# Sharing out a first mixer's work anew: softmax division, conv taps, roots and modulation steps

## The chip, the cores and the metric

The kernel runs on one core of a Trainium2 chip. The metric is the device time of one execution in microseconds (us). The engines are named as the profile names them: PE is the matmul engine (PEld its weight loads), DVE the vector engine, ACT the scalar engine, POOL the GpSimd engine, and SP the engine whose queue issues nearly all DMAs here. Each engine works off its own queue in order; semaphores tie the queues together.

## The reference

Two layers of a diffusion trunk run over 128 context tokens and 512 latent tokens of width 1024, in float32. Layer 0 is a mixer of attention (8 heads, 2 key-value heads, width 64) and a convolution branch; layer 1 is an mLSTM; each is followed by a squared-ReLU MLP. Every sub-layer is modulated by vectors computed from a conditioning vector. What the change touches is the modulation vectors and the mixer of layer 0:

```
m = silu(cond) @ w_ada + b_ada            # 6 vectors of 1024 for each layer
h = x * (1 + scale) + shift
q, k, v, u = split(h @ w_in)              # 512, 128, 128, 1024 columns
q, k = rmsnorm(q), rmsnorm(k)             # per head of 64; latent tokens get rotary positions
p = softmax(q k^T / 8)                    # latent: over 512 latent and 128 cached context keys
att = p v
u = a * sigmoid(gate)                     # a, gate are the halves of u: 512 channels
u = depthwise_conv(u, width 31) + bias
u = silu(layernorm(u))
out = concat(att, u) @ w_out
```

## The kernel before

All products of float32 numbers run as three matmuls on a high and a low part (`mm3`, L193 to L195). Weights come from memory in raw tiles of 512 KB (L149, three buffers); a piece of 128x512 is split by a cast on ACT into `whi` (L166) and a subtraction on POOL into `wlo` (L167). The pairs of `whi` and `wlo` lie in a ring of eight slots.

The program is written with the Tile framework: the code fixes what is computed, and a scheduler with a model of the machine sets the order of each engine's queue when the kernel is built. The conv taps are written with a low priority (`CONV_BEHIND`), so they fill a queue where nothing else is ready.

The first mixer has two stages. In the products (58 to 193 us of the span) the projections are computed in the order of `GEMMS = "01k2qr3"`: glu 0 and 1, the key-value group, glu 2, the q group, the r group (the second half of q), glu 3. Each glu is 128 channels of the conv branch; behind it stand its 31 taps. A tap is either one DVE operation (L965; the first one L956) or an ACT product (L970) with a POOL addition (L972); `CONV_DVE` lists the taps that DVE takes, for four channel tiles of 128: all 31, all 31, eight, four. The k and q groups each have a chain on DVE (sum of squares, L1063; a reciprocal root; scaling, L1067; rotary positions, L1071 to L1080). The root is `rsqrt_here`: a guess from the exponent bits and three Newton rounds of four operations (L400 to L403), 15 operations on tiles of 128x10 or 128x20.

In the attention (193 to 335 us) twelve units (four pairs of heads, each with context tokens and two halves of the latent tokens) run one ahead: scores of the next unit (L1173, L1187), then the values of this one. A softmax is a maximum on DVE (L1152), an exponential with its sum on ACT (L1154), a reciprocal (L1155) and the division on DVE (L1157): 32 divisions of 128x640 and eight of 128x128. Transposes (L1219), their copies (L1222 on ACT, L1224 on DVE) and the products with v (L1226) follow. At unit 8 stands `conv_norm`, the layer norm of the conv branch, which uses the same root. Behind the attention comes out_proj.

A modulation vector is a generator, `ada_steps`: eight steps, each with two loads of 256 KB into a ring pair (L287) and four narrow matmuls into one PSUM bank (L293, which the trace shows as eight records of two kinds), then a DVE addition of the bias (L297) and, unless it is a gate vector, two PE transposes (L305) and four DVE copies (L308); a gate goes to memory (L300). The generators wait in a list, `pending`; `background(n)` runs the first of them n steps on, and `drain()` runs all that are left. Three vectors are queued in the products and seven in the attention, where `background` runs seven steps after each unit and `drain()` the rest at unit 8.

Of the kernel before, what the change touches and what calls it, by code (L numbers as in the profile page):

```python
# [9 lines left out]
F32 = mybir.dt.float32  # L10
F32R = mybir.dt.float32r
I32 = mybir.dt.int32
AF = mybir.ActivationFunctionType
# [5 lines left out]
P = 128  # L19
# [39 lines left out]
LATE_DVE = 0  # L59
CONV_DVE = (range(31), range(31), range(0, 31, 4), range(0, 31, 8))  # L60
PT_ACT = (0,)
# [6 lines left out]
GEMMS = "01k2qr3"  # L68
ADA_IN_ATT = 7
FAST = (1, 3)  # L70
# [22 lines left out]
def trunk_kernel(ctx: ExitStack, tc: tile.TileContext, I, O):  # L93
# [221 lines left out]
    def background(n=1):  # L315

        for _ in range(n):
            while pending:
                try:
# [3 lines left out]
                    pending.pop(0)  # L323

    def drain():
        while pending:
            background()
# [63 lines left out]
    def rsqrt_here(out, var, n, scale):  # L391
# [7 lines left out]
        for _ in range(3):  # L399
            nc.vector.tensor_tensor(out=a, in0=out, in1=out, op=ALU.mult)  # L400
            nc.vector.tensor_tensor(out=a, in0=a, in1=v, op=ALU.mult)
            nc.vector.tensor_scalar(out=a, in0=a, scalar1=-0.5, scalar2=1.5, op0=ALU.mult, op1=ALU.add)
            nc.vector.tensor_tensor(out=out, in0=a, in1=out, op=ALU.mult)  # L403

    def rsqrt_one(r, var):
# [507 lines left out]
    K.ada_raw = ring_raw  # L913
    pending += [ada_vec(0, v) for v in (2, 3, 4)]

    with ExitStack() as m0s:
# [13 lines left out]
        if True:  # L930
# [122 lines left out]
            def chain(x, c0, n):  # L1053
# [10 lines left out]
                rr = smallp.tile([P, NT, n], F32, name=f"rr{n}", bufs=1)  # L1064
                rsqrt_here(
                    rr.rearrange("p t h -> p (t h)"), ss.rearrange("p t h -> p (t h)"), NT * n, 1.0 / HD)
# [35 lines left out]
            def q_group(grp, kn=None):  # L1102
                ws = load_n256(w_in, grp * 256)
                for t in range(NT):
                    ps = ps1()
                    tm_tile(ws, act, t, ps[:, 0:256])
                    nc.scalar.copy(out=qkv[:, t, grp * 256:(grp + 1) * 256], in_=ps[:, 0:256])
                    background(1)
                    if kn is not None:
                        put_k(kn[:, t], t)  # L1110
                chain(0, grp * 256, 4)

            kn = None
            for what in GEMMS:
# [4 lines left out]
                else:  # L1119
                    glu(int(what), 3)  # L1120
            drain()
# [24 lines left out]

        def softmax(ps, dst, multi):

# [7 lines left out]
            d2 = dst.rearrange("p a b -> p (a b)") if multi else dst  # L1156
            nc.vector.tensor_scalar(out=d2, in0=d2, scalar1=ri[:, 0:1], scalar2=None, op0=ALU.mult)  # L1157

# [5 lines left out]
        def weights_of(i, s):  # L1164
# [3 lines left out]
            if s < 0:  # L1168
# [6 lines left out]
                for h in range(2):  # L1175
                    softmax(sp[:, h, 0:P], pp[:, h, :], False)
                Ps[i, s] = pp
                return
            pts = [[], []]
            for t in (1 + 2 * s, 2 + 2 * s):  # L1180
                for h in range(2):
# [7 lines left out]
                    pt = att.tile([P, 2, HT], F32, name="ptok", bufs=PTOK)  # L1189
                    softmax(s2[:, :, 0:HT], pt, True)  # L1190
                    pts[h].append(pt.rearrange("p a b -> p (a b)"))
# [44 lines left out]
        def conv_norm():  # L1236
# [35 lines left out]
            rc = smallp.tile([P, NT], F32, name="rc", bufs=1)  # L1272
            rsqrt_here(rc, pv[:, 0:NT], NT, 1.0)
            for ts in ((0, 1, 2, 3), (4,)):
# [21 lines left out]

        ada_late = [(0, 5)] + [(1, v) for v in range(6)]
        pending += [ada_vec(*x) for x in ada_late[:ADA_IN_ATT]]
        units = [(i, u) for i in range(HEADS // 2) for u in (-1, 0, 1)]
        prep(0)  # L1300
        weights_of(*units[0])
        for n, (i, u) in enumerate(units):
# [6 lines left out]
            if n == NORM_AT:  # L1309
                drain()  # L1310
                for t in range(NT):
# [3 lines left out]
                cl = cls.enter_context(tc.tile_pool(name="cl", bufs=1, side="right", reuse_waits="tile"))  # L1315
                conv_norm()
        cls.close()
    ada_scope.close()
# [80 lines left out]
    with Sub(0) as S:  # L1399
        S.rows(ALPHA)  # L1400
        out_proj(I["w_out_a"][0], S, S.finish_mixer("f0"))
        K.ada_m = lambda: S.fp.tile([P, 256], F32, name="ada_m")
        pending += [ada_vec(*x) for x in ada_late[ADA_IN_ATT:]]
        v_w = []
# [523 lines left out]
```

## Time and profile before

| | us |
|---|---|
| median of 3 runs | 1737.89 (1736.95 to 1741.92) |
| the profiled execution's own time | 1737.0 |
| its span in the trace | 1735.2 |
| products of the first mixer, in the span | 58 to 193 |
| attention | 193 to 335 |

The span reaches from the first to the last instruction that the trace shows. The view by windows gives each engine's busy time, the granted clock of PE and the share of the DMA engines in a stretch; the view by groups sums instructions of one line; the timelines list single instructions with the wait ahead of them and what ended it. A bracket such as `[6.61 <-DVE ada_m L297]` says that the engine stood idle for 6.61 us until DVE's write of `ada_m` by line 297. PE in the span's 40 slices is mostly at 8 or 9 tenths; the chain of waits that ended last begins at 898 us and so tells nothing of the first mixer.

### The profile page before, as it was taken

How to read it: one execution, taken by the hardware profiler on the slowest of the kernel's cores; microseconds unless marked ns; L12 is line 12 of the kernel's file. 1: busy time of each engine (PE TensorE's matmuls, PEld its weight loads, DVE VectorE, ACT ScalarE, POOL GpSimd, SP SyncE). 2: the span in 40 equal slices, each digit the busy share in tenths (PEclk: the TensorE clock that was granted, in tenths of full speed). 3: DMA queues.
4: the chain of work that ended last, by engine and by line, in shares of the span. 5: the costliest groups of instructions: out<-in, count | busy, mean ns of one | idle time of the engine just before them, and what ended most of it. 6: DMA issues, size and time to landing. Idle time of an engine off the chain costs nothing. (4 is left out here: it accounts for less than half of the span.)

```text
span 1735.2 us, 27401 instructions
## 1 busy us (share of the span) xinstructions
PE 1607.3 (93%) x10155; PEld 1412.7 (81%) x10155; DVE 1098.1 (63%) x1924; ACT 796.3 (46%) x1560; POOL 1005.4 (58%) x760
## 2 busy tenths in 40 slices
PE   7988899998989999999788998997989999999996
PEld 4678555898879989987678998897979889989885
DVE  2899997669434444356875687778498354344367
ACT  2224666345444344343543555556265444344343
POOL 2246474247955546548654766756459756546565
PEclk8999999998999999999999999999999999999998
DMA  9852885323432213216223222235442323213241
GB/s 307 256 185 75 268 306 178 71 101 119 130 85 92 92 56 97 86 61 206 83 69 103 71 84 91 98 98 194 123 152 85 125 89 98 89 57 98 85 158 61
DMA packets 151309, 211.76 MB, mean 122 GB/s; under 512 B 11845, under 2 KB 92969, under 8 KB 151176
## 3 DMA queue, kind: packets, MB, share of 16 engines
q1 hardware_dynamic: 150944, 209.94, 37.4%
q8 instruction: 80, 1.31, 0.3%
q14 instruction: 53, 0.43, 0.1%
q10 hardware_dynamic: 232, 0.08, 0.0%
HBM read 186.74 MB, written 23.24 MB: 121 GB/s over the span
## 5 line engine op out<-in xcount | busy, mean ns | idle before, releaser
L167 POOL TENSOR_TENSOR wlo<-raw,whi 128x512 fp32r<-128x512 f32 x374 | 518.6, 1410 | 412.2 <-ACT whi L166 397.5
L166 ACT CAST whi<-raw 128x512 fp32r<-128x512 f32 x368 | 224.7, 620 | 429.2 <-PE ps L195 192.1
L193 PE MATMUL ps<-whi,h 128*128 128x512 f32 x640 | 254.5, 399 | 11.0 <-DVE pr L526 5.7
L194 PE MATMUL ps<-wlo,h 128*128 128x512 f32 x640 | 254.6, 398 | 0.3 <-POOL wlo L167 0.3
L195 PE MATMUL ps<-whi,h 128*128 128x512 f32 x640 | 253.6, 396 | 0.0
L193 PE MATMUL ps<-act_h,whi 128*128 128x320 f32 (+2 forms) x704 | 221.2, 316 | 8.5 <-ACT act_h L625 7.5
L194 PE MATMUL ps<-act_l,whi 128*128 128x320 f32 (+2 forms) x704 | 221.3, 315 | 5.5 <-DVE act_l L626 3.1
L195 PE MATMUL ps<-act_h,wlo 128*128 128x320 f32 (+2 forms) x704 | 220.9, 314 | 2.2 <-POOL wlo L167 2.2
L167 POOL TENSOR_TENSOR wlo<-s,whi 128x512 fp32r<-128x512 f32 x118 | 163.9, 1393 | 67.2 <-ACT whi L166 61.9
L758 DVE TENSOR_TENSOR acc<-acc,ps 128x512 f32<-128x512 f32 x120 | 81.8, 685 | 162.0 <-PE ps L195 162.0
L193 PEld LDWEIGHTS ps<-whi,h 128*128 128x128 f32 x640 | 121.3, 190 | 40.2 <-DVE pr L526 6.0
L193 PEld LDWEIGHTS ps<-act_h,whi 128*128 128x128 f32 x704 | 135.3, 192 | 13.2 <-ACT act_h L625 7.9
L195 PEld LDWEIGHTS ps<-whi,h 128*128 128x128 f32 x640 | 121.3, 190 | 29.2
L194 PEld LDWEIGHTS ps<-wlo,h 128*128 128x128 f32 x640 | 121.5, 190 | 28.1 <-POOL wlo L167 1.2
L194 PEld LDWEIGHTS ps<-act_l,whi 128*128 128x128 f32 x704 | 134.9, 192 | 8.9 <-DVE act_l L626 3.9
L195 PEld LDWEIGHTS ps<-act_h,wlo 128*128 128x128 f32 x704 | 134.9, 192 | 3.1 <-POOL wlo L167 3.1
L193 PE MATMUL ps<-whi,act_h 128*128 128x256 f32 x440 | 126.1, 290 | 0.3 <-DVE acc L1095 0.3
L194 PE MATMUL ps<-wlo,act_h 128*128 128x256 f32 x440 | 124.7, 287 | 0.0
L195 PE MATMUL ps<-whi,act_l 128*128 128x256 f32 x440 | 123.8, 287 | 0.0
L972 POOL TENSOR_TENSOR cy<-cy,tap 128x655 f32<-128x655 f32 x50 | 80.3, 1606 | 54.0 <-DVE cy L965 22.6
L193 PE MATMUL ps<-T_h,whi 128*128 128x320 f32 x336 | 103.7, 309 | 1.6 <-ACT pr L550 1.6
L166 ACT CAST whi<-s 128x512 fp32r<-128x512 f32 x120 | 73.2, 616 | 67.3 <-DVE s L501 54.9
(437 smaller groups left out, 4066.0 us busy)
## 6 DMA issues: line engine op xcount, KB each, us to landing
raw<-in_w_ff_dram SPq DMA_DIRECT2D x128, 512.0 KB
whi<-in_w_ada_dram SPq DMA_DIRECT2D x80, 256.0 KB
wlo<-in_w_ada_dram SPq DMA_DIRECT2D x80, 256.0 KB
raw<-in_w_in_m_dram SPq DMA_DIRECT2D x32, 512.0 KB
ada_w<-in_w_ada_dram SPq DMA_DIRECT2D x32, 256.0 KB
acc_d<-acc SPq DMA_DIRECT2D x15, 512.0 KB
raw<-in_w_in_a_dram SPq DMA_DIRECT2D x12, 512.0 KB
rx<-acc_d SPq DMA_DIRECT2D x20, 256.0 KB
```

What stands on the lines that cost most here:

```text
L166: nc.scalar.copy(out=hv, in_=src)
L167: (eng or nc.gpsimd).tensor_tensor(out=lv, in0=src, in1=f32(hv), op=ALU.subtract)
L193: nc.tensor.matmul(out=out, lhsT=lh, rhs=rh, start=start, stop=False)
L194: nc.tensor.matmul(out=out, lhsT=lh, rhs=rl, start=False, stop=False)
L195: nc.tensor.matmul(out=out, lhsT=ll, rhs=rh, start=False, stop=stop)
L758: nc.vector.tensor_tensor(out=x, in0=x, in1=ps, op=ALU.add)
L972: nc.gpsimd.tensor_tensor(out=y, in0=y, in1=tp, op=ALU.add)
```

## The change

Four edits are made, all on the first mixer, and line numbers move by 1 to about 21.

- Of the taps of channel tile 2 DVE takes 16 instead of eight, and of tile 3 seven instead of four. ACT and POOL have 39 taps instead of 50.
- In each softmax the division of the first head of a pair moves to ACT as a scaled copy; the second head's stays on DVE.
- The root of the k, q and r chains and of `conv_norm` becomes `rsqrt_root`: a square root on ACT, a reciprocal on DVE and one Newton round, five DVE operations instead of 15. ACT's function tables are loaded 12 times in the program instead of seven; the five more lie in the first mixer.
- Six vectors instead of three are queued in the products and four instead of seven in the attention. A tile of the q and r groups runs two steps instead of one, a half of glu 2 and 3 five instead of three; a unit of the attention runs two instead of seven. At unit 8 only a generator that has begun is finished (`settle`), and the rest is drained behind the units.

In SP's queue the second raw tile of the r group and both of glu 3 (512 KB each) stood one after another, eight modulation loads behind the first tile of r. Now 20 modulation loads stand ahead of the first of the three, eight more ahead of the second, and 20 more ahead of the third.

```diff
-CONV_DVE = (range(31), range(31), range(0, 31, 4), range(0, 31, 8))
+CONV_DVE = (range(31), range(31), range(0, 31, 2), range(0, 31, 5))
-ADA_IN_ATT = 7
+ADA_IN_ATT = 2
...
+    def settle():
+
+        if pending and inspect.getgeneratorstate(pending[0]) == inspect.GEN_SUSPENDED:
+            for _ in pending.pop(0):
+                pass
...
+    def rsqrt_root(out, var, n, scale):
+
+        v, y, a = (smallp.tile([P, 20], F32, name=f"rq_{x}", bufs=1)[:, 0:n] for x in "vya")
+        nc.scalar.activation(out=y, in_=var, func=AF.Sqrt, bias=eps_t[:, 0:1], scale=scale)
+        nc.vector.tensor_scalar(out=v, in0=var, scalar1=scale, scalar2=EPS, op0=ALU.mult, op1=ALU.add)
+        nc.vector.reciprocal(out=y, in_=y)
+        nc.vector.scalar_tensor_tensor(out=a, in0=y, scalar=-0.5, in1=y, op0=ALU.mult, op1=ALU.mult)
+        nc.vector.tensor_tensor(out=a, in0=a, in1=v, op=ALU.mult)
+        nc.vector.scalar_tensor_tensor(out=out, in0=a, scalar=1.5, in1=y, op0=ALU.add, op1=ALU.mult)
...
-    pending += [ada_vec(0, v) for v in (2, 3, 4)]
+    ada_late = [(0, 5)] + [(1, v) for v in range(6)]
+    pending += [ada_vec(0, v) for v in (2, 3, 4)] + [ada_vec(*x) for x in ada_late[:3]]
...
-                rsqrt_here(
+                rsqrt_root(
                     rr.rearrange("p t h -> p (t h)"), ss.rearrange("p t h -> p (t h)"), NT * n, 1.0 / HD)
...
-                    background(1)
+                    background(2)
                     if kn is not None:
                         put_k(kn[:, t], t)
...
-                    glu(int(what), 3)
+                    glu(int(what), 3 if what in "01" else 5)
...
-            nc.vector.tensor_scalar(out=d2, in0=d2, scalar1=ri[:, 0:1], scalar2=None, op0=ALU.mult)
+            if on_act:
+                nc.scalar.activation(out=d2, in_=d2, func=AF.Copy, scale=ri[:, 0:1])
+            else:
+                nc.vector.tensor_scalar(out=d2, in0=d2, scalar1=ri[:, 0:1], scalar2=None, op0=ALU.mult)
...
-                    softmax(s2[:, :, 0:HT], pt, True)
+                    softmax(s2[:, :, 0:HT], pt, True, h == 0)
...
-            rsqrt_here(rc, pv[:, 0:NT], NT, 1.0)
+            rsqrt_root(rc, pv[:, 0:NT], NT, 1.0)
...
-        ada_late = [(0, 5)] + [(1, v) for v in range(6)]
-        pending += [ada_vec(*x) for x in ada_late[:ADA_IN_ATT]]
+        pending += [ada_vec(*x) for x in ada_late[3:]]
...
             if n == NORM_AT:
-                drain()
+                settle()
...
                 conv_norm()
+        drain()
         cls.close()
...
-        pending += [ada_vec(*x) for x in ada_late[ADA_IN_ATT:]]
```

Two places of the queues show what moves. The first is DVE in the key-value chain, before; `rh_a` and `rr` belong to the root, `cy` is the conv sum, `up` the gated input of the conv, `ada_m` a modulation vector.

```order
79 L403 TENSOR_TENSOR rr_1143<-rh_a,rr_1143 128x10
80 L965 SCALAR_TENSOR_TENSOR cy<-up,cw,cy 128x655
81 L400 TENSOR_TENSOR rh_a<-rr_1143 128x10
82 L965 SCALAR_TENSOR_TENSOR cy<-up,cw,cy 128x655
83 L401 TENSOR_TENSOR rh_a<-rh_a,rh_v 128x10
84 L965 SCALAR_TENSOR_TENSOR cy<-up,cw,cy 128x655
85 L402 TENSOR_SCALAR rh_a<-rh_a 128x10
86 L981 SCALAR_TENSOR_TENSOR up<-sg,ps_1267 128x320
87 L297 TENSOR_TENSOR ada_m<-psc,ada_m 128x256
88 L965 SCALAR_TENSOR_TENSOR cy<-up,cw,cy 128x655
89 L403 TENSOR_TENSOR rr_1143<-rh_a,rr_1143 128x10
```

In the changed kernel the same stretch of DVE's queue reads as follows (`rq_a` and `rq_y` are the new root's tiles):

```order
68 L418 SCALAR_TENSOR_TENSOR rq_a<-rq_y 128x10
69 L983 SCALAR_TENSOR_TENSOR cy<-up,cw,cy 128x655 x2
70 L419 TENSOR_TENSOR rq_a<-rq_a,rq_v 128x10
71 L983 SCALAR_TENSOR_TENSOR cy<-up,cw,cy 128x655 x2
72 L420 SCALAR_TENSOR_TENSOR rr_1143<-rq_a,rq_y 128x10
73 L999 SCALAR_TENSOR_TENSOR up<-sg,ps_1182 128x128
74 L999 SCALAR_TENSOR_TENSOR up<-sg,ps_1182 128x192
75 L983 SCALAR_TENSOR_TENSOR cy<-up,cw,cy 128x655
76 L1085 TENSOR_TENSOR acc<-acc,rr_1143 128x5x128
77 L983 SCALAR_TENSOR_TENSOR cy<-up,cw,cy 128x655
78 L298 TENSOR_TENSOR ada_m<-psc,ada_m 128x256
```

Before, the root is in its second and third rounds when the addition L297 comes, with a tap between any two operations; now the root has ended and the scaling (L1085) has begun ahead of the addition (now L298).

The second place is PE at the start of the q group, before; `ps1_1477` is its second tile, and L305 the transposes of a modulation vector:

```order
520 L195 MATMUL ps1_1477<-whi_1422,act_l_90 128x256
521 L193 MATMUL ps1_1477<-whi_1422,act_h_89 128x256
522 L194 MATMUL ps1_1477<-wlo_1423,act_h_89 128x256
523 L195 MATMUL ps1_1477<-whi_1422,act_l_90 128x256
524 L305 MATMUL psc_1333<-ident_75,ada_m_1055 128x128 x2
525 L193 MATMUL ps1_1477<-whi_1426,act_h_89 128x256
526 L194 MATMUL ps1_1477<-wlo_1427,act_h_89 128x256
```

In the changed kernel the transposes (now L306) and the first q tile, `ps1_1469`:

```order
493 L196 MATMUL ps2_1296<-act_h_89,wlo_1169 128x320
494 L306 MATMUL psc_1272<-ident_75,ada_m_1055 128x128 x2
495 L194 MATMUL ps1_1469<-whi_1451,act_h_89 128x256
496 L195 MATMUL ps1_1469<-wlo_1452,act_h_89 128x256
497 L196 MATMUL ps1_1469<-whi_1451,act_l_90 128x256
498 L194 MATMUL ps1_1469<-whi_1451,act_h_89 128x256
499 L195 MATMUL ps1_1469<-wlo_1452,act_h_89 128x256
```

And a few rows further on, with the second tile `ps1_1538`, transposes of the k group (L1064, L1065) and modulation matmuls (L294):

```order
505 L195 MATMUL ps1_1538<-wlo_1452,act_h_89 128x256
506 L196 MATMUL ps1_1538<-whi_1451,act_l_90 128x256
507 L1064 MATMUL po_1531<-identr_501,ks_1527 128x128
508 L1065 MATMUL po_1531<-identr_501,ks_1527 128x128
509 L1064 MATMUL po_1531<-identr_501,ks_1527 128x128
510 L1065 MATMUL po_1531<-identr_501,ks_1527 128x128
511 L194 MATMUL ps1_1469<-whi_1455,act_h_89 128x256
512 L194 MATMUL ps1_1538<-whi_1455,act_h_89 128x256
513 L294 MATMUL psc_1283<-whi_1284,stat_109 32x256 x2
514 L294 MATMUL psc_1283<-wlo_1285,stat_109 32x256 x2
515 L294 MATMUL psc_1283<-whi_1345,stat_109 32x256 x2
516 L294 MATMUL psc_1283<-wlo_1346,stat_109 32x256 x2
```

Before, the transposes stood six matmuls into the second q tile, behind a first tile computed whole. Now they stand ahead of all q tiles, right behind the last matmul of glu 2 (`ps2_1296`), and the first two q tiles go on together, one weight piece after another, with modulation steps between the pieces.

## Rows read from the trace of the kernel before

**Rows 1.** The page's busy time of the engines, whole span:
```profile
PE 1607.3 (93%) x10155; PEld 1412.7 (81%) x10155; DVE 1098.1 (63%) x1924; ACT 796.3 (46%) x1560; POOL 1005.4 (58%) x760
```

**Rows 2.** Windows; stretch, its length, busy us of each engine, clock, DMA share, GB/s:
```profile
58.00:193.00 135.00, 116.30 (x920) 101.31 (x922) 129.76 (x203) 45.06 (x91) 63.79 (x43) 0.95 0.53 174
193.00:335.00 142.00, 136.65 (x1061) 83.54 (x1054) 120.25 (x252) 89.87 (x186) 64.58 (x46) 0.98 0.63 208
```

**Rows 3.** Timeline of PE at 121 to 131; start, duration, in brackets the wait:
```profile
129.73 0.69 PE L305 MATMUL psc<-ident,ada_m 128*128 128x128 f32 x2 [6.61 <-DVE ada_m L297]
```

**Rows 4.** Timeline of DVE, 117 to 131:
```profile
123.06 1.97 DVE L965 SCALAR_TENSOR_TENSOR cy<-up,cw,cy 128x655 f32<-128x655 f32 x1
126.10 0.89 DVE L965 SCALAR_TENSOR_TENSOR cy<-up,cw,cy 128x655 f32<-128x655 f32 x1
126.91 0.15 DVE L400 TENSOR_TENSOR rh_a<-rr 128x10 f32<-128x10 f32 x1
129.25 0.42 DVE L297 TENSOR_TENSOR ada_m<-psc,ada_m 128x256 f32<-128x256 f32 x1
```

**Rows 5.** Timeline of POOL, 117 to 131:
```profile
116.87 9.28 POOL L167 TENSOR_TENSOR wlo<-raw,whi 128x512 fp32r<-128x512 f32 x6
```

**Rows 6.** Windows around the large wait:
```profile
90.00:122.00 32.00, 31.73 (x273) 27.49 (x266) 32.00 (x44) 8.97 (x18) 13.76 (x10) 1.00 0.50 167
122.00:138.00 16.00, 9.39 (x64) 9.19 (x63) 16.00 (x26) 4.86 (x8) 9.42 (x7) 0.79 0.33 100
```

**Rows 7.** Timeline of PE, 229 to 236:
```profile
230.25 0.41 PE L293 MATMUL psc<-whi,stat 128*32 128x256 f32 x2
...
232.22 0.39 PE L293 MATMUL psc<-whi,stat 128*32 128x256 f32 x2
```

**Rows 8.** PE's groups, attention; count, busy, mean ns, idle before, releaser:
```profile
L293 PE MATMUL psc<-whi,stat 128*32 128x256 f32 x190 | 28.4, 399 | 1.1 <-issue 1.1
L305 PE MATMUL psc<-ident,ada_m 128*128 128x128 f32 x8 | 1.6, 286 | 0.9 <-DVE ada_m L297 0.9
```

**Rows 9.** Timeline of PE at the products' end, 181 to 193:
```profile
185.32 0.63 PE L1187 MATMUL ps<-kTA,qT 128*128 128x320 f32 x1 [2.38 <-DVE up L981]
```

**Rows 10.** Waits of SP's queue, 58 to 200; total us, times, longest:
```profile
SPq L287 <- PE ps L195: 28.1, 13, 7.8
```

**Rows 11.** DVE's groups in the products, 58 to 193:
```profile
L965 DVE SCALAR_TENSOR_TENSOR cy<-up,cw,cy 128x655 f32<-128x655 f32 x65 | 70.1, 1100 | 0.5
L402 DVE TENSOR_SCALAR rh_a<-rh_a 128x20 f32<-128x20 f32 (+1 forms) x9 | 4.8, 536 | 0.2
L401 DVE TENSOR_TENSOR rh_a<-rh_a,rh_v 128x20 f32<-128x20 f32 (+1 forms) x9 | 4.8, 533 | 0.1
L400 DVE TENSOR_TENSOR rh_a<-rr 128x20 f32<-128x20 f32 (+1 forms) x9 | 3.8, 424 | 0.2
L403 DVE TENSOR_TENSOR rr<-rh_a,rr 128x20 f32<-128x20 f32 (+1 forms) x9 | 3.7, 409 | 0.1
```

**Rows 12.** All taps of line 965; duration ns least/median/most:
```profile
L965 DVE SCALAR_TENSOR_TENSOR cy<-up,cw,cy x70: 879/895/2005, 63.0 to 258.5; 128x655 f32<-128x655 f32 x70
```

**Rows 13.** ACT's groups, 58 to 335:
```profile
L970 ACT ACTIVATE tap<-up,cw 128x655 f32<-128x655 f32 x50 | 41.9, 841 | 36.1 <-POOL cy L972 28.6 <-DVE up L981 7.5
L1154 ACT ACTIVATE ptok<-ps,nm 128x640 f32<-128x640 f32 x32 | 25.5, 797 | 15.5 <-DVE nm L1152 6.9 <-PE ps L1219 5.9 <-DVE rh_a L401 2.0
```

**Rows 14.** Timelines of PE and of DVE at the end of the attention:
```profile
324.63 0.39 PE L193 MATMUL ps<-whi,act_h 128*128 128x256 f32 x1
...
331.83 1.50 DVE L1295 TENSOR_TENSOR act_l<-cy,act_h 128x512 fp32r<-128x512 f32 x3 [0.23 <-ACT act_h L1294]
```

**Rows 15.** DVE's groups in the attention, 193 to 335:
```profile
L1157 DVE TENSOR_SCALAR ptok<-ptok,ri 128x640 f32<-128x640 f32 x32 | 28.7, 896 | 0.5
```

**Rows 16.** Timeline of ACT, 895 to 906, in the second layer:
```profile
902.18 1.28 ACT L1572 ACT_TABLE_LOAD   x1
903.48 0.83 ACT L1572 ACTIVATE g_ab<-g_ab,one_t 64x640 f32<-64x640 f32 x1
```

More of the change, by code (lines that the diff above doesn't have):

```diff
@@ L1 @@
+import inspect
 from contextlib import ExitStack
@@ L1145, in prep, with softmax @@
             qTs[i] = qT
-        def softmax(ps, dst, multi):
+        def softmax(ps, dst, multi, on_act):
             nm = smallp.tile([P, 1], F32, name="nm")
@@ L1175, in weights_of @@
                 for h in range(2):
-                    softmax(sp[:, h, 0:P], pp[:, h, :], False)
+                    softmax(sp[:, h, 0:P], pp[:, h, :], False, h == 0)
                 Ps[i, s] = pp
```

## The prediction

> **What bounds the kernel now.** I read the page's busy times first [rows 1]: PE is busy for 93% of the span, but that mean covers stages with different limits. So I cut the span at the borders of the first mixer [rows 2]. In the products (58 to 193 us) DVE works 129.76 of 135 us and PE 116.30: DVE is the tighter engine there, and PE waits for it. In the attention (193 to 335 us) it is the other way round, PE 136.65 of 142 and DVE 120.25. The two stages need two sums. An instruction taken from PE in the attention counts in full, one added to PE in the products may hide in its waits, and one taken from DVE counts in the products as far as DVE's queue as a whole gets shorter.
>
> The largest wait of PE in the products ends at 129.73 us [rows 3]: two transposes, L305, have waited 6.61 us for a DVE addition, L297, and PE's queue, q tiles included, stood behind them. The DVE timeline says why the addition came so late [rows 4]: it stands at 129.25, behind a file of conv taps (L965) and small operations of the reciprocal root (L400 to L403) that stretched, a tap to 1.97 us, while POOL ran six subtractions from 116.87 to 126.15 [rows 5]; once POOL was done a tap took 0.89 and a small operation 0.15. The clock granted in the 16 us around this wait is 0.79; in the 32 us ahead, where PE was busy for 31.73, it is 1.00 [rows 6]. So the stall costs more than its 6.61 us.
>
> **The change part by part.**
>
> *Modulation steps.* 24 of the 56 steps that the attention runs (three vectors of eight) move into the products. Where steps follow each other in the attention, a group of four records starts every 0.22 us (230.25 to 232.22 is nine intervals) [rows 7]; a step is two such groups, 0.44 us, and 24 give 10.5 us. The sum over the stage gives the other bound: 28.4 us for 190 records of the `whi` half, 0.149 each, four to a step, 0.60 us and 14.3 us in all [rows 8]. I take 10.5, since the steps that go come from the middle units; the opening of the attention keeps the same two vectors' worth in the new order. Two of the three vectors also take two transposes each with them, 0.29 us a record, and a part of their waits of 0.9 [rows 8]: 0.9 us more. Together -11.4 us where PE is the bound.
>
> In the products the same 10.5 to 14.3 us come onto PE. All 24 stand behind the q group's start in the new order, so behind 122 us. From there on PE waits 6.61 us [rows 3], 2.38 us at 185 [rows 9], and several other times; over the whole stage it has 18.7 us free [rows 2]. The steps fit, and I cost them at nothing as long as DVE is what ends the stage. If no wait takes them in, they cost 10.5 to 14.3.
>
> *What the steps do to the queues.* With them go 48 loads of 256 KB, 12.6 MB: over 135 us that is 93 GB/s on top of 174, at a DMA share that would rise from 0.53 to about 0.81 [rows 2], so there is room. But these weights use the same eight slots as the weights of q, r and glu, and SP issues all loads in order. SP's waits in this stage [rows 10] show loads of modulation weights (L287) held back by PE (13 times, 28.1 us, at most 7.8). Now the raw weights of the r group and of glu 3 stand behind more modulation loads. The cost lies between nothing (PE has other tiles) and one longest wait for each of three groups, 3 x 7.8 = 23.4 us. I take one mean wait, 28.1/13 = 2.2 us, since the q group's first tiles are now computed piece by piece, as weights arrive.
>
> *Roots.* In the three chains of the products each root goes from 15 DVE operations to five, and one on ACT, for whose round trip conv taps stand ready on DVE. The four forms of a Newton round took 3.7 + 4.8 + 4.8 + 3.8 = 17.1 us for 36, 0.475 each [rows 11]; 30 fewer are -14.3 us of DVE (by the undisturbed 0.15 us of [rows 4], -4.5). The conv norm's ten fewer lie in the attention, off the bound: 0.
>
> *Taps.* 11 taps come to DVE: 11 x 1.10 us, the mean of the 65 [rows 11], is +12.1; the fastest of all took 0.879 and the slowest 2.005 [rows 12], so 9.7 to 22.1. Additions for three more vectors at 0.42 us [rows 4] and their copies, together eight small operations of at least 0.15, add about 2.6. DVE's sum in the products is -14.3 + 12.1 + 2.6 = +0.4, which I take as nothing, with bounds of -2.0 and +20.2 (short root operations together with slow taps). The stage keeps its length. The page "SBUF — State Buffer" of the Trainium skill, section "Who interferes with whom", states that a DVE operation with two SBUF inputs and a GpSimd operation that reads SBUF exclude each other for a whole instruction; it speaks against taps on DVE. The trace agrees as to the effect (1.97 us beside the subtractions, 0.89 behind them [rows 4, 5]), but the mean of 1.10 says that one tap in five meets it. Were all 11 caught, as that rule allows, the stage would be 9.9 us longer, 11 x (2.005 - 1.10).
>
> POOL loses 11 additions and ACT 11 products of 0.84 us [rows 13]. The conv chain ends earlier, and with it the conv norm; but its tail is hidden already: out_proj's matmuls run from 324.63 on, and DVE is at the norm until 333.3 [rows 14]. So: 0.
>
> *Softmax division.* 20 of 40 leave DVE, 16 x 0.896 us [rows 15] and four small ones. ACT gets them at about 0.80 us, its duration for the exponential of the same shape [rows 13], 13 us in all, of which the taps give back nine. Both engines stay below PE: DVE near 102 us, ACT near 96 of 142. So 0; were half of the 16 wide divisions to stand in the way of an exponential that PE waits for, 8 x 0.8 = 6.4 us.
>
> *Table loads.* The first mixer gets five more. A load takes 1.28 us and the next ACTIVATE starts right behind it [rows 16]. Four lie where ACT has spare time. The one ahead of glu 3's gate stands on the path to the DVE product L981 for which PE waited at 185 [rows 9]: +1.3. The page "ScalarE: Activation LUTs" of the Trainium skill, section "What ACT_TABLE_LOAD costs", adds a drain of 1380 ns to each load; the rows leave no room for one (a load ends at 903.46, its ACTIVATE starts at 903.48). By the page this term would be 2.7 us and the sum 1.4 us higher.
>
> *Sum.* From the profiled execution's own 1737.0 us (span 1735.2, and 1.8 outside it; the median of the runs is 1737.89): -11.4 + 2.2 + 1.3 = -7.9, so **1729 us**. Behind 335 us the order hardly changes: 0.
>
> **The rivals.**
> 1. *The steps come back.* The products lengthen by what the attention loses, because PE's waits stand at other places than the steps: 10.5 us return, 1739.6 by the whole sum, 1736.1 without the terms for queue and table. For it: PE works in order, and much of its idle time lies in a few long waits. Against it: DVE needs 129.8 us in any case.
> 2. *The large wait goes too.* In the new order DVE's addition stands right behind a root of five operations, and the transposes behind all of glu 2's matmuls. Then the 6.61 us go, and with the clock at 0.79 for 16 us [rows 6] up to 3 more: 1729.1 - 9.6 = 1719.5. Against it: DVE's sum gets no shorter, so the wait may only move to the end of the stage.
> 3. *Weights late: slower.* A modulation load at the head of SP's queue waits until PE frees a slot, the raw weights of q, r and glu 3 wait behind it, PE starves at each group's start and frees no slots meanwhile, and DVE's chains get their input late. By the longest wait [rows 10] this is 23.4 us in place of 2.2: 1750. From 16.2 us on, 5.4 a group, it is slower by a measurable amount (1729.1 - 2.2 + 16.2 = 1743.1). For it: the raw weights of r and glu 3 were loaded well ahead, and no longer are. Against it: glu 2's weights lie among modulation steps already, and PE was busy for 31.73 of 32 us there [rows 6].
> 4. *The attention waits for softmax.* With fewer steps between the units, PE meets the chain of score, maximum, exponential, division and transpose bare, and ACT's divisions lie on it: the 6.4 us above, 1735.5.
>
> **How the numbers follow.** Likeliest is the sum, 0.40, with a range of its own of 1723 to 1734. Rival 1: 0.18; rival 2: 0.15; rival 3: 0.15; rival 4: 0.12. A measurement of this kernel can tell about 0.3% from no change, 5.2 us: faster is below 1732.7, slower above 1743.1. Faster: 0.37 of the likeliest, 0.02, 0.15, 0 and 0.03 of the rivals in order, 0.57. Slower: 0.03 of rival 1 and 0.13 of rival 3, 0.16. Within: 0.27. The range reaches down to 1718, below rival 2, and up to 1743, with rivals 1 and 4 inside; most of rival 3 and the edge of rival 2 are left out, about 0.2.
>
> **What would show it.** Right: the attention's stage about 11 us shorter with PE still busy for over 95%; about twice as many records of the modulation matmuls in the products; the transposes behind glu 2 waiting under 2 us near 125; products of 132 to 140 us; no wait of PE for `wlo` over 3 us at the starts of q and r. Wrong: PE waiting for `wlo` there (rival 3), products 10 us longer with more idle time of DVE (1), a shorter DVE sum and products under 128 us (2), or PE below 93% in the attention with waits for `ptok` (4).

## The result, and the profile after

The changed kernel took 1750.14 us (median of 12 runs, 1742.22 to 1753.57), the kernel before 1739.38 beside it (12 runs): a ratio of 1.0056, 95% interval 1.004 to 1.0072. It is slower by about 10 us, where 8 us faster had been forecast. The profiled execution of the changed kernel was the fastest of its twelve, 1742.22 us with a span of 1740.4; a second profile, of an execution of 1752.21 us, is used below where they differ.

The border between products and attention is put at PE's first latent score (L1187 before, L1208 now), 185.3 us before and 195.4 now, and the end of the attention at out_proj's first matmul, 324.6 and 329.2. By this border the windows of the kernel before are, in the columns of [rows 2]:

```profile
58.00:185.30 127.30, 111.73 (x890) 98.86 (x888) 122.26 (x194) 41.00 (x83) 59.06 (x41) 0.96 0.52 169
185.30:324.60 139.30, 130.82 (x1000) 75.61 (x1000) 119.25 (x246) 87.08 (x181) 68.02 (x48) 0.96 0.62 214
```

and of the changed kernel:

```profile
58.00:195.40 137.40, 128.77 (x1083) 103.52 (x1081) 128.05 (x196) 47.60 (x94) 62.80 (x44) 1.00 0.74 244
195.40:329.20 133.80, 115.39 (x810) 74.16 (x809) 102.16 (x208) 94.48 (x198) 51.59 (x34) 0.89 0.43 138
```

The products grew from 127.3 to 137.4 us, and the attention shrank only from 139.3 to 133.8. In the products PE's busy time rose by 17.0 us and its idle time fell by 6.9, from 15.6 to 8.6; in the attention PE is busy for 86% and its clock fell from 0.96 to 0.89. The second profiles of both kernels give the same picture: 127.9 and 142.4 before, 138.9 and 136.0 after, with PE's idle time in the products at 16.3 and 6.2 us.

The groups of PE in the products (to the first latent score) show what came there:

```profile
L294 PE MATMUL psc<-whi,stat 128*32 128x256 f32 x190 | 27.3, 386 | 2.3 <-issue 1.6 <-DMA whi<-in_w_ada_dram 0.7
L294 PE MATMUL psc<-wlo,stat 128*32 128x256 f32 x192 | 26.2, 386 | 0.3 <-DMA wlo<-in_w_ada_dram 0.2
L306 PE MATMUL psc<-ident,ada_m 128*128 128x128 f32 x8 | 1.5, 271 | 0.0
```

Before, there were 98 and 100 such records. The 92 more of each are the moved steps (four of each to a step), at 386 ns a record as before. The two kinds run side by side, so their busy times do not add up; the windows of all records that read `stat`, of before and of the changed kernel, count both kinds once:

```profile
58.00:185.30 127.30, 15.32 (x198) 5.54 (x198) 0.00 (x0) 0.00 (x0) 0.96 0.52 169
58.00:195.40 137.40, 33.46 (x382) 11.82 (x382) 0.00 (x0) 0.00 (x0) 1.00 0.74 244
```

The moved steps brought 18.1 us of PE's time into the products. PE's waits there, before,

```profile
PE psc L305 <- DVE ada_m L297: 6.6, 1, 6.6
PE po L1046 <- DVE kTB L1051: 2.1, 1, 2.1
PE ps L195 <- POOL wlo L167: 1.6, 1, 1.6
PE po L1046 <- DVE ks L1042: 1.4, 1, 1.4
```

add up, with three shorter ones, to 12.9 us, of which 10.6 are waits for DVE. In the changed kernel they are 8.6 us, of which 3.1 are waits for DVE; DVE itself is idle for 9.4 us in place of 5.0. The transposes, which had waited 6.61 us [rows 3], wait no more. Where that stall stood, PE now shows four short ones:

```profile
123.51 0.41 PE L294 MATMUL psc<-whi,stat 128*32 128x256 f32 x2 [1.62 <-issue]
...
131.38 0.41 PE L294 MATMUL psc<-wlo,stat 128*32 128x256 f32 x2 [0.24 <-DMA wlo<-in_w_ada_dram]
...
133.55 0.39 PE L195 MATMUL ps<-wlo,act_h 128*128 128x256 f32 x1 [1.53 <-POOL wlo L168]
...
136.59 0.39 PE L194 MATMUL ps<-whi,act_h 128*128 128x256 f32 x1 [0.56 <-ACT acc L1125]
```

The window of 122 to 138 us answers to [rows 6]: PE busy for 12.16 us of 16 and at the full clock.

```profile
122.00:138.00 16.00, 12.16 (x117) 8.71 (x118) 15.96 (x29) 7.33 (x19) 10.33 (x5) 1.00 0.74 232
230.00:250.00 20.00, 15.95 (x92) 10.56 (x91) 17.96 (x43) 17.91 (x41) 11.98 (x8) 0.81 0.25 83
300.00:320.00 20.00, 10.46 (x80) 6.23 (x79) 18.49 (x29) 12.45 (x29) 11.68 (x8) 0.77 0.50 140
```

Its two other rows are the attention's bad places. From 300 to 320 PE was busy for 10.46 of 20 us at a clock of 0.77. The timeline of PE there:

```profile
304.79 0.65 PE L1247 MATMUL po<-pT,vS 128*64 128x256 f32 x4 [2.34 <-DVE pT L1245]
...
315.56 1.12 PE L1247 MATMUL po<-pT,vS 128*64 128x256 f32 x4 [7.20 <-DVE act_l L1183]
```

PE stood 7.20 us for the DVE instruction L1183, which empties the output of the third pair of heads. The timeline of DVE shows what that instruction stood behind:

```profile
298.69 2.11 DVE L1310 TENSOR_SCALAR cy<-cy,hgb 128x655 f32<-128x655 f32 x2
300.73 1.92 DVE L1312 SCALAR_TENSOR_TENSOR cy<-csq,cy 128x655 f32<-128x655 f32 x1
...
306.49 3.16 DVE L1312 SCALAR_TENSOR_TENSOR cy<-csq,cy 128x655 f32<-128x655 f32 x2
...
313.33 1.48 DVE L1316 TENSOR_TENSOR act_l<-cy,act_h 128x512 fp32r<-128x512 f32 x3
314.74 0.68 DVE L1183 TENSOR_TENSOR act_l<-po,act_h 128x512 fp32r<-128x512 f32 x1
```

and the timeline of POOL what ran beside it:

```profile
299.03 9.92 POOL L168 TENSOR_TENSOR wlo<-raw,whi 128x512 fp32r<-128x512 f32 x6 [45.22 <-ACT whi L167]
309.27 2.73 POOL L168 TENSOR_TENSOR wlo<-raw,whi 128x512 fp32r<-128x512 f32 x2 [0.32 <-ACT whi L167]
```

L1310, L1312 and L1316 are the tail of the conv norm. Before, it ran from 323.9 to 333.3 us, behind the last unit and beside out_proj [rows 14]. Now the norm's matmuls begin 32 us earlier (257.3, before 289.3). Some 18 of these come from the conv chain (POOL's last addition ends at 253.8, before at 271.6); the others come from the modulation steps ahead of the norm, since it begins 3.5 us behind that addition, before 17.7 (2.6 in the run with the steps alone, 21.8 in the one with all but the steps). So the tail lies in DVE's queue ahead of the last two units, and runs beside POOL's subtractions of out_proj's weights: an L1312 took 1.6 us in the mean, before 0.83.

On DVE and ACT the prices came out near the estimates. The groups of DVE, with the taps and one of the new root's operations in the products, and the divisions and L1312 in the attention:

```profile
L983 DVE SCALAR_TENSOR_TENSOR cy<-up,cw,cy 128x655 f32<-128x655 f32 x75 | 80.3, 1095 | 6.1 <-POOL cy L990 5.5
L420 DVE SCALAR_TENSOR_TENSOR rr<-rq_a,rq_y 128x20 f32<-128x20 f32 (+1 forms) x3 | 1.6, 546 | 0.1
```

```profile
L1178 DVE TENSOR_SCALAR ptok<-ptok,ri 128x640 f32<-128x640 f32 x16 | 11.0, 685 | 0.3
L1312 DVE SCALAR_TENSOR_TENSOR cy<-csq,cy 128x655 f32<-128x655 f32 x4 | 6.4, 1615 | 0.0
```

and of ACT, with its divisions and the loads of the root's table:

```profile
L1176 ACT ACTIVATE ptok<-ptok,ri 128x640 f32<-128x640 f32 x16 | 13.2, 826 | 2.9 <-DVE ri L1173 2.9
L415 ACT ACT_TABLE_LOAD x3 | 3.8, 1283 | 0.1
```

A tap is at 1.095 us as before [rows 11], the divisions that stayed on DVE at 0.685 instead of 0.896 [rows 15], those of ACT at 0.826. In the timeline of ACT at the products' end the load stands where ACT has nothing else to do:

```profile
182.74 1.28 ACT L995 ACT_TABLE_LOAD   x1
186.10 0.44 ACT L995 ACTIVATE sg<-ps 128x320 f32<-128x320 f32 x1 [2.09 <-PE ps L196]
```

ACT had waited 2.09 us more for PE when its gate operation began: the load cost nothing there.

Waits for `ptok`, the sign of rival 4, are there in the attention, but small: PE waited 2.5 us in all for ACT's exponentials (L1172) and not for its divisions, against the 7.20 for L1183.

### The profile page after: what moved, and what is told of

Same layout as the page of the kernel before. It is cut to its first block, busy times and chain, and to the rows that moved or that the text cites. A ratio compares the mean times of both kernels' runs of the same rounds, so it can differ in the third digit from the quotient of the medians.

```text
span 1740.4 us, 27339 instructions
## 1 busy us (share of the span) xinstructions
PE 1609.0 (92%) x10155; PEld 1414.6 (81%) x10155; DVE 1090.6 (63%) x1875; ACT 806.7 (46%) x1578; POOL 993.3 (57%) x749
## 4 chain that ended last, share of the span: by engine, by line
PE 60%; DVE 19%; DMA 9%; POOL 5%; ACT 3%; issue 3%; SPq 1%; DVEq 0%; POOLq 0%; ACTq 0%
PE ps L194 17%; PE ps L195 17%; PE ps L196 17%; DVE cy L983 3%; DMA raw<-in_w_in_m_dram 3%; POOL wlo L168 3%; DMA ada_w<-in_w_ada_dram 2%; DMA raw<-in_w_ff_dram 1%; PE po L1247 1%; PE ps L1240 1%; DVE act_l L643 1%; DVE wt L1705 1%; PE psu L194 1%; PE psu L195 1%; PE psu L196 1%
## 5 line engine op out<-in xcount | busy, mean ns | idle before, releaser
L194 PE MATMUL ps<-whi,h 128*128 128x512 f32 x640 | 253.5, 398 | 10.1 <-DVE pr L543 3.9
L196 PE MATMUL ps<-whi,h 128*128 128x512 f32 x640 | 253.8, 397 | 0.0
L516 DVE TENSOR_TENSOR s<-raw 128x512 f32<-128x512 f32 x40 | 50.0, 1249 | 96.9 <-DMA raw<-in_w_ff_dram 58.4
```

The costliest lines, as they stand in the source:

```text
L194: nc.tensor.matmul(out=out, lhsT=lh, rhs=rh, start=start, stop=False)
L196: nc.tensor.matmul(out=out, lhsT=ll, rhs=rh, start=False, stop=stop)
L516: tt(out=s3, in0=m11, in1=m21, op=ALU.subtract)
```

## The experiments

The expectations speak of two explanations. Theory A: the moved steps fill PE in the products, where too little idle time takes them in, and the conv norm's tail comes to stand ahead of the last units. Rival R puts the loss down to ACT's divisions and table loads. All ratios are to runs of the kernel before on the same chip. The times by border (first latent score, out_proj's first matmul) are of one profile each.

| run | ratio, 95% interval | first latent score | out_proj | attention |
|---|---|---|---|---|
| before, two profiles | | 185.3, 185.9 | 324.6, 328.3 | 139.3, 142.4 |
| changed, two profiles | 1.0056 (1.004 to 1.0072) | 195.4, 196.9 | 329.2, 332.9 | 133.8, 136.0 |
| steps alone | 1.0096 (1.0076 to 1.0116) | 201.4 | 340.3 | 138.9 |
| all but the steps | 1.0010 (0.9996 to 1.0023) | 185.3 | 326.6 | 141.3 |
| changed, tail late | 1.0011 (0.9992 to 1.003) | 196.0 | 324.0 | 128.0 |
| changed, thin steps | 1.0026 (1.0008 to 1.0044) | 192.0 | 326.3 | 134.3 |
| one vector, tail late | 1.0126 (1.0103 to 1.0148) | 186.2 | 330.2 | 144.0 |
| no vector, tail late | 1.0101 (1.0078 to 1.0124) | 185.3 | 327.5 | 142.2 |
| changed, subtraction on POOL | 1.0046 (1.0032 to 1.006) | 196.3 | 330.2 | 133.9 |
| changed, tail late and that | 1.0013 (0.9999 to 1.0027) | 196.2 | 325.1 | 128.9 |
| changed, taps as before | 1.0047 (1.0029 to 1.0064) | 193.2 | 332.0 | 138.8 |
| changed, roots as before | 1.0099 (1.0082 to 1.0116) | 198.9 | 336.9 | 138.0 |

**The steps alone.** The kernel before with the edits to `pending`, `background`, `ADA_IN_ATT` and `settle` only:

```diff
-ADA_IN_ATT = 7
+ADA_IN_ATT = 2
...
-    pending += [ada_vec(0, v) for v in (2, 3, 4)]
+    pending += [ada_vec(0, v) for v in (2, 3, 4)] + [ada_vec(*x) for x in ada_late[:3]]
...
-                drain()
+                settle()
```

> The kernel before with the modulation edit alone (24 steps moved into the products, two steps a unit in the attention, no drain ahead of the conv norm). Theory A (the moved steps fill PE in the products, about 0.6 us each with little idle time to take them in, and the conv norm's tail comes to stand ahead of the last units in DVE's queue): products about 10 us longer, attention 3 to 8 us shorter, in all 3 to 8 us slower than before. Rival R (the steps are harmless, and ACT's divisions and table loads make the loss in the attention): not slower, 0 to 8 us faster.

It was 1.0096, slower than A had said: the products are 16.1 us longer and the attention by 0.4 shorter. R is refuted as the whole cause, since neither divisions nor tables are in it.

**All but the steps.** The changed kernel with those edits undone.

> The changed kernel with the modulation steps where they were before; taps, divisions and roots changed. Theory A: the products no longer than before or up to 5 us shorter, the attention about as before, in all between 5 us faster and 2 us slower than before. Rival R: the loss stays, 5 to 10 us slower than before.

1.0010, as A expected. The products are as long as before to a tenth of a us, with the stall at L305 down from 6.61 [rows 3] to 2.57:

```profile
124.81 0.28 PE L1064 MATMUL po<-identr,ks 128*128 128x128 f32 x1 [1.86 <-DVE ks L1060]
...
129.26 0.69 PE L306 MATMUL psc<-ident,ada_m 128*128 128x128 f32 x2 [2.57 <-DVE ada_m L298]
```

The wait of 1.86 us ahead of it, and others, took its place. So taps, divisions and roots together are worth nothing without the steps; with the steps they are worth the difference of 1.0096 and 1.0056, of which 4.5 to 6.0 us lie in the products (143.4 us with the steps alone, 138.9 and 137.4 with all four edits).

**The tail late.** The conv norm's tail is written behind the units, and its scale is made with an operand from the last softmax, so that it can't run ahead:

```diff
-                conv_norm()
+                hgb = conv_norm()
+        conv_tail(hgb)
...
+        def conv_tail(hgb0):
+            nc.vector.tensor_scalar(out=zero, in0=lastp[-1][:, 0:1], scalar1=0.0, scalar2=None, op0=ALU.mult)
+            nc.vector.tensor_scalar(out=hgb, in0=hgb0, scalar1=zero[:, 0:1], scalar2=None, op0=ALU.add)
```

> The changed kernel with the conv norm's tail (the last two of its three DVE steps, its tanh and its splits) tied to the last softmax, so that it stands among the last two units on DVE, as before the change. Theory A: PE's waits of 7.2 and 2.3 us near 305 and 316 us go, with the half clock around them: 7 to 11 us faster than the changed kernel, 1740 to 1743 by the medians, about as before. Rival R: within 2 us of the changed kernel.

1744.2 us by the median, 8 us less than the changed kernel beside it (1752.1) and 2 above the kernel before. The attention is 128.0 us, 11.3 shorter than before the change. PE's wait of 7.20 us for L1183 is 0.8 there. The windows of the attention and DVE's timeline show the tail among the copies of the last units, and each L1322 (the former L1312) at 0.83 us:

```profile
196.00:324.00 128.00, 113.57 (x809) 73.04 (x808) 98.43 (x210) 94.82 (x198) 49.40 (x34) 0.92 0.41 142
```

```profile
315.74 0.83 DVE L1322 SCALAR_TENSOR_TENSOR cy<-csq,cy 128x655 f32<-128x655 f32 x1
...
317.02 0.68 DVE L1246 COPY pT<-ps 128x512 f32<-128x512 f32 x1
...
317.82 0.84 DVE L1322 SCALAR_TENSOR_TENSOR cy<-csq,cy 128x655 f32<-128x655 f32 x1
```

**The changed kernel again**, for a second profile.

> The changed kernel once more, for a profile nearer to its median: its first profile was of the fastest of twelve runs (1742.2 against a median of 1750.1). Theory A: the same order of waits with more half clock in the attention's second half, 230 to 330 us. Rival R: the additional time lies in waits for ACT.

1752.1 us by the median (8 runs). Neither expectation names what it showed. The attention was 136.0 us, and behind out_proj it took 1417.5 us, against 1411.2 in the first profile. It begins with one DVE instruction in the first MLP, L516, a subtraction of two 128x512 tiles, that took 9.8 us longer; some 3 us of this are made good behind it. In the first profile, on DVE:

```profile
440.48 3.00 DVE L516 TENSOR_TENSOR s<-raw 128x512 f32<-128x512 f32 x1 [3.57 <-DMA raw<-in_w_ff_dram]
```

in the second, on DVE:

```profile
444.44 12.80 DVE L516 TENSOR_TENSOR s<-raw 128x512 f32<-128x512 f32 x1 [3.63 <-DMA raw<-in_w_ff_dram]
457.17 0.81 DVE L739 TENSOR_TENSOR h<-c,h 128x640 fp32r<-128x640 f32 x1
```

and POOL beside it:

```profile
443.96 2.92 POOL L643 TENSOR_TENSOR act_l<-h,act_h 128x1280 fp32r<-128x1280 f32 x1
446.81 5.00 POOL L168 TENSOR_TENSOR wlo<-raw,whi 128x512 fp32r<-128x512 f32 x4
451.77 1.27 POOL L462 TENSOR_TENSOR rx<-rx,lnt 128x512 f32<-128x512 f32 x1
452.99 2.49 POOL L168 TENSOR_TENSOR wlo<-raw,whi 128x512 fp32r<-128x512 f32 x2
455.42 1.27 POOL L462 TENSOR_TENSOR rx<-rx,lnt 128x512 f32<-128x512 f32 x1
```

POOL ran nine instructions without a gap from 443.96 to 456.69 us, and DVE's instruction, begun 0.48 us behind the first of them, ended 0.55 us behind the last. Seven of the profiled executions have this order of POOL (behind the first instruction four subtractions, a step of the residual, two subtractions and another step): the two of the changed kernel, the tail late, the thin steps, one vector, no vector and the old roots. In three of them (the second of the changed kernel, the tail late, the thin steps) the instruction took 12.54 to 13.14 us, in four 2.9 to 3.2. Five others have another order there, with a step of the residual behind the first subtraction: the two of the kernel before, the steps alone, all but the steps, and the old taps. In them it took 1.4 to 2.3 us. It is not all that differs behind out_proj: all but the steps and the steps alone, without the long instruction, took 1417.4 and 1420.0 us there, and the tail late, with it, 1430.3.

**The thin steps.** Of each moved vector the six middle steps multiply 32 of 256 columns, so 18 of 24 steps need little of PE while loads, slots and order stay. The kernel leaves the products of the other 224 columns out, so it is no version of the program:

```diff
+            nn = 32 if thin and 0 < k < KT - 1 else 256
...
-                    out=ps[32 * j:32 * (j + 1), 0:256], lhsT=stat[:, 2 * k:2 * k + 32],
+                    out=ps[32 * j:32 * (j + 1), 0:nn], lhsT=stat[:, 2 * k:2 * k + 32],
```

> The changed kernel, but of the 24 moved steps the middle six of each vector multiply only 32 of their 256 columns; loads, slots, waits and the order stay, so only PE's time for 18 of the 24 steps goes (the rest of those columns is left out of the sums). Theory A (the products are bound by PE once the steps are there, about 0.6 us a step): the first latent scores come 7 to 10 us earlier than in the changed kernel, near 187 us. Rival Q (loads and slots of the ring, not PE's time, cost the 10 us): they come within 3 us of the changed kernel's 195 to 197 us.

The first latent score came at 192.0 us, 3.4 and 4.9 earlier than in the two profiles of the changed kernel: between A's 7 to 10 and Q's 3. The busy time of the modulation matmuls fell by 10.3 us, from 33.46 to 23.12. Both theories fall short; in the middle of the products DVE is then busy nearly all the time, and PE's clock is lower:

```profile
122.00:165.00 43.00, 35.92 (x372) 31.46 (x372) 42.72 (x61) 20.00 (x41) 25.52 (x18) 0.88 0.80 258
```

DVE is busy for 42.72 of 43 us there, where the changed kernel has 39.65 and a clock of 1.00 instead of 0.88. So neither PE nor DVE alone sets the length; the two are within some 5 us of each other. What loads and slots have in the rest, this run does not separate.

**One vector moved, and none, with the tail late.**

```diff
-ADA_IN_ATT = 2
+ADA_IN_ATT = 6
...
-    pending += [ada_vec(0, v) for v in (2, 3, 4)] + [ada_vec(*x) for x in ada_late[:3]]
+    pending += [ada_vec(0, v) for v in (2, 3, 4)] + [ada_vec(*x) for x in ada_late[:1]]
...
```

> One vector of eight steps moved in place of three (two steps a tile of q and r, three a glu half, six a unit of the attention), with the conv norm's tail tied to the last softmax. Theory A: PE's idle time in the products takes in 4 us of 5, the attention gets 3.8 us shorter: 2 to 6 us faster than before, 1735 to 1740. Rival Q: any moved vector costs a queue wait at q, 1741 or more.

> No vector moved (the steps as before the change), taps, divisions and roots as changed, the conv norm's tail tied to the last softmax. Theory A: the tail's place costs 2 to 4 us there too (a few copies stood behind it), so out_proj begins 2 to 4 us earlier than at 326.6 us, and the whole is 0 to 4 us faster than before. Rival R (divisions on ACT cost the attention 2 us): out_proj begins at 326 us still.

1.0126 and 1.0101, far from what was expected. With one vector the products are 0.9 us longer than before, so PE took in most of its eight steps, as A said (their busy time there went from 15.3 to 21.9 us); but the attention is 4.7 us longer instead of 3.8 shorter, with a wait of 5.45 us for the addition of a modulation vector in its opening. Both runs lose about 12 us elsewhere, at the end of the second layer, where DVE in both orders waits for the load of a gate; in the run without a moved vector:

```profile
1243.65 0.42 DVE L468 TENSOR_TENSOR s<-ps,h 128x256 f32<-128x256 f32 x1 [6.74 <-DMA h<-gate_d]
1251.36 1.09 DVE L468 TENSOR_TENSOR s<-ps,h 128x256 f32<-128x256 f32 x3 [7.29 <-DMA h<-gate_d]
```

The kernel before has no such wait. For the first mixer the runs say this: with no vector moved the late tail does not help (out_proj at 327.5, at 326.6 without it), so its place hurts only where the attention has lost its steps. Rival R's 2 us for the divisions fit both runs without moved steps (attention of 141.3 and 142.2 us, before 139.3), but the second profile of the kernel before has 142.4. Why the gate's load comes late in both is not shown; the edits do not touch it.

**The kernel before again.**

> The kernel before once more, for a second profile. Behind out_proj the profiles so far took 1410.6 us (before), 1411.2 and 1417.5 (changed) and up to 1430.3 (tail tied late), where one VectorE addition of a weight preparation took 2 us in some and 12.5 in others. If that is chance and no effect of the change, this profile may show it too, or another length behind out_proj; if the change brings it, it shows 2 to 3 us and 1410 to 1412.

1744.3 us; behind out_proj 1414.2 us, with the instruction above at 2.34 us. So executions of one kernel differ by 3 to 4 us behind out_proj, and by as much in the attention, without that instruction.

**The subtraction on POOL.**

```diff
-                tt(out=s3, in0=m11, in1=m21, op=ALU.subtract)
+                (nc.gpsimd.tensor_tensor if K.nup in (1,) else tt)(out=s3, in0=m11, in1=m21, op=ALU.subtract)
```

> The changed kernel, with one subtraction of 128x512 in the first MLP's weight preparation (the DVE instruction that took 3.0 us in one profile of the changed kernel and 12.8 in the other) put on POOL, where it stands among POOL's own instructions. Theory S (that DVE instruction often waits until POOL's unbroken run of nine instructions ends, and the change's new order behind out_proj brought that about): 4 to 7 us faster than the changed kernel by the medians, 1743 to 1747; nothing changes ahead of out_proj. Rival N (chance, hidden by other waits): within 2 us of the changed kernel.

1747.4 us (1745.5 to 1748.4), 7.1 above the kernel before beside it, where the changed kernel was 10.8 and 10.3 above its own. That is 3 to 4 us by the medians, but the interval of its ratio overlaps that of the changed kernel: the sign is not settled by it. Its profile shows 1413.9 us behind out_proj.

**Both repairs.**

> Both repairs together: the conv norm's tail tied to the last softmax and that subtraction on POOL. Theories A and S: out_proj near 324 us and no long subtraction near 437 us, 1735 to 1740, 1 to 5 us faster than before. Without S: as with the tail alone, about 1744.

1740.9 us against 1740.4: level with the kernel before, and no better. With the tail late, the subtraction's place makes no difference that can be told (1.0011 and 1.0013).

**Taps, and roots, as before.** The changed kernel with the old `CONV_DVE`, and with `rsqrt_here`.

> The changed kernel with the taps shared as before (eight and four on DVE). If PE is the bound of the products once the steps are there, the first latent scores stay within 2 us of 195 to 197 us. If DVE is the bound, they come 4 to 10 us earlier, since 11 taps of 0.9 to 1.1 us go from DVE's queue. The conv chain ends later, so the conv norm's tail stands less far ahead of the last units and the attention gets 2 to 5 us shorter by theory A.

> The changed kernel with the roots as before, of 15 DVE instructions. If DVE is the bound of the products, the first latent scores come 5 to 14 us later than 195 to 197 us; if PE is the bound and the roots only delay single waits, 0 to 4 us later. The table loads of the root go too: by 1.3 to 6 us of ACT in the attention nothing should change.

Without the moved taps the first latent score came 2.2 to 3.7 us earlier, just outside what a pure PE bound allows; the time is that of the changed kernel. Against the expectation the attention got longer, 138.8 us. With the old roots the score came 2.0 to 3.5 us later and the attention took 138.0 us: 1.0099. The table loads of the root are gone in that run, and it is no faster: they are not what the attention loses. Of 14 us that the roots take off DVE, a quarter or less is seen in the products, and about as much in the attention's opening (first product with v 25.6 us behind the first latent score, 21.9 in the changed kernel).

## Why the prediction was wrong

**The moved steps in the products: the step that failed first.** The prediction costed them "at nothing as long as DVE is what ends the stage". The products got 10.1 us longer (11.0 by the second profiles), and it was the steps: 16.1 us with the steps alone, 0.0 with all but the steps. The working that looked safe set 10.5 to 14.3 us of steps against 18.7 us of PE's idle time, and both were off. The upper bound counted the records of `whi` alone, by [rows 8]; with both kinds the moved steps took 18.1 us. And of the 18.7 us only 15.6 lie ahead of the first latent score. So not even all of PE's idle time would have held them, and 6.9 us of it (10.1 by the second profiles) took work in. The condition failed with it: PE's waits for DVE went from 10.6 to 3.1 us, PE is busy for 94% of the stage, and DVE's idle time rose, so DVE alone no longer ends it. The length and the sign are rival 1's (10.5 us, more idle time of DVE), its reason only in part: the large wait did take work in, and there was more work than idle time.

**The steps out of the attention: the right number, in part by luck.** -11.4 us was the term, and with the tail kept late the attention is 11.3 us shorter (10.4 with both repairs; against the second profile of before 14.4 and 13.5). But an instruction taken from PE did not count in full there: PE's busy time fell by 17.3 us, from 130.82 to 113.57, and its idle time rose by 6. PE is busy for 89% in place of the 95% that was to show it.

**The tail of the conv norm: the step that failed second.** "Its tail is hidden already ... So: 0." It was hidden because it came last. A conv norm that was ready 32 us earlier took the cover away: the scheduler put the tail ahead of the last two units, where PE waits for DVE. By the medians it is worth 8 us, by the profiles 5.2 to 8.9 at out_proj's start. No rival had it; the order of the changed kernel, in which eight copies of the last units stand behind the tail and before none, had shown it.

**Behind 335 us: "0" was too little.** By the first profiles it is 0.6 us, by the second ones 3.3, and the long DVE instruction is in three of seven profiles with the new order of POOL, in none of five with another. What it is worth in the median, some 3 us, is inferred from medians whose intervals overlap, and with the tail late no difference can be told.

**Queue and table.** The 2.2 us for weights that come late showed as waits of 1.53 and 0.24 us in the q group, so this size was about right and rival 3 did not happen: in SP's queue (58 to 200 us) the modulation loads waited 58 us for PE, before 45, while the raw weights waited 16, before 35, and PE's waits for weights grew by about 1 us. The table load that was put on the path at 1.3 us had 2.09 us of ACT's idle time behind it: 0. As to the drain that the Trainium skill adds there ("ScalarE: Activation LUTs", "What ACT_TABLE_LOAD costs"), these rows cannot tell, since ACT waited for PE after the load. Two other loads of the changed kernel, at 151.78 and 281.94 us, can: the root follows each at once, so no drain shows there.

```profile
151.78 1.28 ACT L415 ACT_TABLE_LOAD   x1
153.07 0.31 ACT L415 ACTIVATE rq_y<-ss,eps_t 128x20 f32<-128x20 f32 x1
```

**Roots, taps and division.** Nothing in the products, as the prediction had it, as long as the steps stay: the run without the steps has them at the length of before. With the steps there they take back 4.5 to 6.0 of the 16.1 us. That the large stall only moves to other waits was said under rival 2, and is what that run's timeline shows.

**Sum.** Against the first profiles, products +10.1, attention -5.5 (-11.3 and 5.8 given back to the tail), behind out_proj +0.6: +5.2 us, which is 1742.2 less 1737.0. The medians differ by 10.8, some 5 us more. The second profile, near the median, has 3.7 us more at out_proj's start and 6.3 more behind it; the second one of the kernel before has 3.7 and 3.6 more too, so how much of this belongs to the change stays open but for the long instruction.

## What to carry to other kernels

Before costing moved work at nothing because an engine is idle, compare the busy time of all its records with the idle time of exactly the stretch that it goes to, and do not expect all of that to be used: here 18.1 us came to 15.6 us of idle time, 6.9 to 10.1 of it took work in, and the stage grew by 10.1. A third of the steps made it 0.9 us longer, so the price is not proportional. Whoever shortens a chain that was hidden should ask where a scheduler will put its end: work that came last for free may come early and stand ahead of work that somebody waits for. After a change, look for long single instructions far behind it before putting the rest down to chance.

## What the runs showed of the hardware

A DVE subtraction with both inputs in SBUF waited through nine POOL instructions in a row, 12.8 us instead of 2 to 3, when POOL had no gap in its queue; in another execution of the same program it got in between the first and the second. The Trainium skill ("SBUF — State Buffer", "Who interferes with whom") tells that the engine which issues first blocks the other for its whole instruction. The trace agrees as to the blocking; here DVE waited out all nine, where in four other profiles with the same order it took 2.9 to 3.2 us.

PE's granted clock is a mean of two levels, 1.00 (2.4 GHz) and 0.50 (1.2 GHz). With fewer steps between the units it fell to 0.81 between 230 and 250 us, where PE was busy for 15.95 of 20 us, and to 0.77 between 300 and 320, where it was busy for 10.46. Before the change it was 1.00 and 0.91 there:

```profile
230.00:250.00 20.00, 18.98 (x187) 10.13 (x185) 19.72 (x40) 15.05 (x35) 14.93 (x10) 1.00 0.88 309
300.00:320.00 20.00, 19.76 (x140) 14.83 (x138) 15.34 (x42) 7.17 (x16) 0.00 (x0) 0.91 0.00 1
```

So not all the time is gained that PE has less work. How much of the attention the clock kept back, no run here separates.
